# Values and states of a chunked recurrence in tiles of their own, one 128-partition state update for two heads

## The chip, the cores and the metric

One core of one Trainium2 chip runs the whole program in a single launch. The metric is the device time of the program in microseconds. Three plain runs of the kernel before are shown, and one profiled execution whose rows are quoted below.

## What is computed

The program is one mixer layer over 2048 tokens of width 1024: an adaptive norm, a wide input projection, three token mixers, an output projection with residual, and a last norm. The change touches the two mixers that are gated linear recurrences, with four heads each. GLA has keys of 64 and values of 128 per head, HGRN keys and values of 64. In chunks of 64 tokens each head does

```python
o_c = einsum('ts,sv->tv', scores, v_c) + einsum('td,dv->tv', q_c * exp(b_cum), state)
state = exp(b_last)[:, None] * state + einsum('sd,sv->dv', k_c * exp(b_last - b_cum), v_c)
```

where `b_cum` is the running sum of the log decay in the chunk and `scores` are the causal, decayed products of queries and keys. The third mixer, a stick-breaking attention, is not touched.

## The kernel before

The program runs in stages: the norm and the first projections, the value projections, the forget projections, the stick-breaking attention with projections woven in, the recurrences, and the output projection. All products are float32, or three products of split float32r parts. Between stages features, values and outputs lie in DRAM.

The recurrence stage (`gla_fast`, `gla_tail`, called from line 1057) works on pairs of heads: pairs 0 and 1 are GLA, pairs 2 and 3 HGRN, taken in this order. A pair's 2048 tokens go in four groups of 512, that is eight chunks, so there are 16 groups, called group 0 to group 15 below; groups 0 to 7 are GLA, 8 to 15 HGRN. Head h of a pair has its features on partitions 64h to 64h+63.

For one group SyncE loads the decays `bc`, queries `qt` and keys `kt`, the values `Vn` in token order, and the values once more into the tiles `W` (lines 884 to 886, 812, 821, 822). ScalarE makes exponentials (894, 897, 902). VectorE makes the scaled queries `eP` and keys `eN` (898, 899, 903), GpSimd the decayed keys `kd` (904). TensorE forms the scores `scp` (914) and transposes `kd` into `ptk` (833). ScalarE copies both out, as `S` and `KTt`, and GpSimd masks `S` into the tile `M` (921).

`W[h]` of a head has 128 partitions and one block per chunk: on its own 64 partitions the values of the chunk, on the other 64 the state at the chunk's start. `M[:, h]` matches it: on the own 64 partitions the masked scores, on the other 64 the queries times their decay, which VectorE writes there across the halves, one head at a time (906). So one product over 128 rows gives a chunk's output for one head (867). The state's increments `U` are 64-row products (844), in two PSUM tiles, one for even and one for odd chunks. VectorE carries the states from chunk to chunk, one instruction for each head and chunk (855), and the last chunk's goes into block 0 of the next group's `W`. The decay of a chunk stands on the swapped halves in `SX`, which two small copies (529 to 531) fill earlier, where the decays are made.

TensorE's order is written out by hand: for group i the scores and transposes, nine products of a gate projection as filler (257), the increments U of group i, nine fillers, the outputs o of group i-1. One of the two filler slots is

```python
            for i, tail in enumerate(gla_fast(GLA_ORDER, gp, gr_, pp, scp)):
                next(tail)
                run(fill, GLA_F[0])
                next(tail)
```

The order on the other engines and on the DMA queues comes from a planner that simulates the program. `U` has one buffer, so U of group i waits until the state updates of group i-1 have read it. `W` has two, so the values of group i+2 are loaded after the outputs of group i. A second, exact path (`gla_exact`) runs only when the decays are extreme; in these runs it is not entered.

Of the kernel before, what the change touches and what calls it, by code (L numbers as in the profile page):

```python
# [8 lines left out]
F32 = mybir.dt.float32  # L9
# [33 lines left out]
def hybrid_mixer_kernel(ctx, tc, x, c, w_ada, b_ada, w_in, w2, bg, gnw, lbl, hnw,  # L43
# [50 lines left out]
    SE = const.tile([P, 4, T // GTF, 3 * NBF], F32, name="SE")  # L94
    SX = const.tile([P, 4, T // GTF, NBF], F32, name="SX")
    ada_b = const.tile([P, 16], F32, name="ada_b")
# [423 lines left out]
    def decay_sums(pr, n, bc, g, s):  # L520

        b3 = v3(bc)
        sm, se = SM[:, pr, n, :], SE[:, pr, n, :]
        nc.vector.tensor_tensor_scan(bc, rmask, g, 0.0, op0=ALU.mult, op1=ALU.add)
        nc.vector.tensor_copy(sm[:, 0:2 * NBF].rearrange("p (e n) -> p n e", e=2),
                              b3[:, :, CB // 2 - 1:CB:CB // 2])
        nc.vector.tensor_tensor(sm[:, 2 * NBF:3 * NBF], sm[:, NBF:2 * NBF], sm[:, 0:NBF], op=ALU.subtract)
        fe[0] = nc.scalar.activation(se, sm, AF.Exp, scale=s)
        for h in range(2):
            nc.vector.tensor_copy(SX[(1 - h) * 64:(2 - h) * 64, pr, n, :],  # L530
                                  SE[h * 64:(h + 1) * 64, pr, n, NBF:2 * NBF])
# [272 lines left out]

    def load_values(pools, pr, g, GT, Wn):
        gla = pr < 2
# [6 lines left out]

        def new_w():
            return [pools.tile([P, NB, dv], F32, tag=f"W{h}", name=f"W{h}", bufs=2) for h in range(2)]
        W = Wn if Wn is not None else new_w()
        if Wn is None:
            nc.gpsimd.memset(W[0][64:128, 0, :], 0.0)
            nc.gpsimd.memset(W[1][0:64, 0, :], 0.0)
        vr = vcols.rearrange("(n p) d -> p n d", p=CB)  # L820
        nc.sync.dma_start(W[0][0:64], vr[:, :, 0:dv])
        nc.sync.dma_start(W[1][64:128], vr[:, :, dv:2 * dv])
        return Vn, W, new_w() if g + 1 < T // GT else None

    def gla_tail(gr_, pp, pr, g, GT, M, kd, dec, Vn, W, Wn):
        gla = pr < 2
# [13 lines left out]
        for n in range(NB):  # L840
            rs = slice((n % 2) * 64, (n % 2) * 64 + 64)
            for h in range(2):
                orow = slice((1 - h) * 64, (1 - h) * 64 + 64)
                mm(U[n % 2][orow, n // 2, :], KTt[rs, n // 2, h * 64:(h + 1) * 64],  # L844
                   Vn[rs, n // 2, h * dv:(h + 1) * dv], start=True, stop=True)
        for n in range(NB):
            for h in range(2):
                orow = slice((1 - h) * 64, (1 - h) * 64 + 64)
                if n + 1 < NB:
                    dst = W[h][orow, n + 1, :]  # L850
                elif Wn is not None:
                    dst = Wn[h][orow, 0, :]
                else:
                    continue
                nc.vector.scalar_tensor_tensor(dst, W[h][orow, n, :], dec[orow, n:n + 1],  # L855
                                               U[n % 2][orow, n // 2, :],
                                               op0=ALU.mult, op1=ALU.add)
        yield


        no = 2 if gla else 1
        o = pp.tile([P, no, GT], F32, tag="o", name="o")
        for n in range(NB):
            ns = slice(n * CB, (n + 1) * CB)
            for h in range(2):
                dst = o[:, h, ns] if gla else o[h * 64:(h + 1) * 64, 0, ns]
                mm(dst, W[h][:, n, :], M[:, h, ns], start=True, stop=True)
        for a in range(no):
# [5 lines left out]
    def gla_fast(pairs, gp, gr_, pp, scp):  # L874

        for pr in pairs:
            gla = pr < 2
            j = pr % 2
            s = 1.0 / 16.0 if gla else 1.0
            Wn = None  # L880
            for g in range(T // GTF):
# [4 lines left out]
                nc.sync.dma_start(kt, s_feat["ka" if gla else "kb"][j][:, tsl])  # L886
                Vn, W, Wn = load_values(gr_, pr, g, GTF, Wn)
# [4 lines left out]
                M = gr_.tile([P, 2, GTF], F32, tag="M", name="M", bufs=3)  # L892
                eP = gp.tile([P, GTF], F32, tag="eP", name="eP")
# [25 lines left out]
                for h in range(2):  # L919
                    hs = slice(h * 64, (h + 1) * 64)  # L920
                    nc.gpsimd.affine_select(v3(M[hs, h, :]), v3(S[hs]),
                                            pattern=[[0, NBF], [1, CB]], base=0,
                                            channel_multiplier=-1, compare_op=ALU.is_ge, fill=0.0)
                yield gla_tail(gr_, pp, pr, g, GTF, M, kd, SX[:, pr, g, :], Vn, W, Wn)

    def gla_exact(gp, pp):
# [4 lines left out]
        nc.sync.dma_start(mx, masks)  # L931
        M = gp.tile([P, 2, GT + NB], F32, name="M")
        nc.gpsimd.memset(M, 0.0)
        for pr in (2, 3, 0, 1):
            gla = pr < 2
            j = pr % 2
            s = 1.0 / 16.0 if gla else 1.0
            Wn = None
            for g in range(T // GT):
# [7 lines left out]
                nc.sync.dma_start(qt, s_feat["qa" if gla else "qb"][j][:, tsl])  # L947
                Vn, W, Wn = load_values(gp, pr, g, GT, Wn)
                if gla:
# [15 lines left out]
                def level(Xk, Xq, mi):  # L965
                    sc = pp.tile([P, NB, CB], F32, tag="sc", name="sc")
                    for n in range(NB):
                        for h in range(2):
                            hs = slice(h * 64, (h + 1) * 64)
                            ns = slice(n * CB, (n + 1) * CB)  # L970
                            mm(sc[hs, n, :], Xk[hs, ns], Xq[hs, ns], start=True, stop=True)
                    for h in range(2):
                        hs = slice(h * 64, (h + 1) * 64)
                        nc.vector.copy_predicated(
                            v3(M[hs, h, 0:GT]), mx[hs, mi:mi + 1, :].broadcast_to((64, NB, CB)), sc[hs])

# [21 lines left out]
                nc.vector.tensor_tensor(kt, kt, dd, op=ALU.mult)  # L998
                for h in range(2):
                    nc.vector.tensor_copy(M[(1 - h) * 64:(2 - h) * 64, h, :], Qs[h * 64:(h + 1) * 64, :])  # L1000
                dec = gp.tile([P, NB], F32, tag="dec", name="dec")
                for h in range(2):
                    orow = slice((1 - h) * 64, (2 - h) * 64)
                    nc.vector.tensor_copy(dec[orow], M[orow, h, GT:GT + NB])
                for _ in gla_tail(gp, pp, pr, g, GT, M, kt, dec, Vn, W, Wn):
                    pass
# [308 lines left out]
```

## Time and profile before

| | |
|---|---|
| three runs | 1293.93, 1297.98, 1299.10 us, median 1297.98 |
| the profiled execution | 1298.31 us, its span 1296.3 us |
| TensorE busy | 1216.6 us, 94% of the span |
| VectorE, ScalarE, GpSimd busy | 742.1, 471.7 and 164.7 us |
| mean granted TensorE clock | 0.977 of full speed |

The profiled execution took 2.0 us more than its span, and lies 0.3 us above the median of the runs. Busy shares are means over stages with different limits; the rows below look at the recurrence stage, from about 869 to 1066 us of the span, where all the changed instructions but two small copies run.

### The profile page before, as it was taken

Reading aid. Unit: us, or ns where it says so; the run is one execution under the profiler, and the core shown is the slowest. Engines: PE = TensorE matmul, PEld = TensorE weight load, DVE = VectorE, ACT = ScalarE, POOL = GpSimd, SP = SyncE. Lnnn points to the kernel's source line nnn. Section 1 sums busy time; section 2 is a strip of 40 time slices with the busy share of each in tenths; the row PEclk is TensorE's granted clock in tenths of the full one; section 3 lists DMA queues with packets and bytes.
Section 4 is the critical chain, followed back from the end, with each engine's and each line's share of the span. In section 5 each row is a group of like instructions: output and inputs, shape, how many; then the busy total and the mean of one; then the engine's idle time right before and its main releaser. Section 6 shows DMA issues by size and latency. Waiting matters only on the chain.

```text
span 1296.3 us, 22081 instructions
## 1 busy us (share of the span) xinstructions
PE 1216.6 (94%) x8682; PEld 987.1 (76%) x8682; DVE 742.1 (57%) x1268; ACT 471.7 (36%) x860; POOL 164.7 (13%) x197
## 2 busy tenths in 40 slices
PE   7999999999999899999999999998978896999997
PEld 6777789899997667777777776766867674777775
DVE  4856325700019873535546488867786667765652
ACT  3376423421124432323223344543333433253621
POOL 3210000000004300000000001012341312000000
PEclk8999999999999999999999999998989897999999
DMA  9765432422123331222333322127977657464621
GB/s 266 237 238 184 143 116 91 150 83 78 54 98 114 131 99 59 78 86 71 99 86 92 110 62 79 33 86 223 266 218 199 196 171 237 134 225 133 203 82 51
DMA packets 177566, 173.73 MB, mean 134 GB/s; under 512 B 39625, under 2 KB 131882, under 8 KB 177454
## 3 DMA queue, kind: packets, MB, share of 16 engines
q1 hardware_dynamic: 144970, 128.70, 33.6%
q10 hardware_dynamic: 32484, 43.54, 9.7%
q8 instruction: 70, 1.15, 0.4%
q14 instruction: 42, 0.34, 0.1%
HBM read 113.47 MB, written 58.73 MB: 133 GB/s over the span
## 4 chain that ended last, share of the span: by engine, by line
PE 61%; DVE 13%; DMA 7%; issue 5%; ACT 2%; POOL 1%; SPq 0%; ACTq 0%; POOLq 0%; DVEq 0%
PE acc L151 5%; PE av L747 5%; PE acc L153 5%; PE acc L152 5%; PE acc L163 4%; PE acc L165 4%; PE acc L164 4%; PE pt L735 4%; PE y L1191 4%; PE y L1189 4%; PE y L1190 4%; PE acc L257 4%; DVE W L855 2%; DVE f L731 2%; DMA kt<-s_kb 2%
## 5 line engine op out<-in xcount | busy, mean ns | idle before, releaser
L731 DVE TENSOR_TENSOR_SCAN f<-f 128x512 f32<-128x512 f32 (+3 forms) x160 | 169.9, 1091 | 21.6 <-ACT f L725 12.1
L151 PE MATMUL acc<-hTh,whi 128*128 128x512 f32 x400 | 161.9, 406 | 8.0 <-ACT st L182 3.8
L152 PE MATMUL acc<-hTl,whi 128*128 128x512 f32 x400 | 159.4, 398 | 0.0
L153 PE MATMUL acc<-hTh,wlo 128*128 128x512 f32 x400 | 159.2, 399 | 0.0
L163 PE MATMUL acc<-whi,hTh 128*128 128x256 f32 (+1 forms) x512 | 145.3, 284 | 1.6 <-ACT stt L190 1.6
L165 PE MATMUL acc<-whi,hTl 128*128 128x256 f32 (+1 forms) x512 | 144.9, 283 | 0.0
L164 PE MATMUL acc<-wlo,hTh 128*128 128x256 f32 (+1 forms) x512 | 144.8, 283 | 0.0
L257 PE MATMUL acc<-hTh,whi 128*128 128x512 f32 x240 | 104.3, 435 | 1.8 <-ACT hTh L241 1.8
L257 PE MATMUL acc<-hTl,whi 128*128 128x512 f32 x240 | 98.1, 409 | 3.9 <-DVE hTl L247 3.8
L1189 PE MATMUL y<-wh,hTh 128*128 128x512 f32 x256 | 101.5, 397 | 0.0
L1190 PE MATMUL y<-wl,hTh 128*128 128x512 f32 x256 | 101.1, 396 | 0.0
L1191 PE MATMUL y<-wh,hTl 128*128 128x512 f32 x256 | 99.9, 395 | 1.0 <-DVE hTl L1157 1.0
L725 ACT ACTIVATE f<-zt 128x512 f32<-128x512 f32 (+3 forms) x160 | 82.0, 537 | 50.5 <-DVE f L731 23.0
L257 PE MATMUL acc<-hTh,wlo 128*128 128x512 f32 x240 | 98.3, 410 | 1.0 <-POOL wlo L271 1.0
L151 PEld LDWEIGHTS acc<-hTh,whi 128*128 128x128 f32 x400 | 75.4, 189 | 29.8 <-ACT st L182 5.1
L163 PEld LDWEIGHTS acc<-whi,hTh 128*128 128x128 f32 x512 | 96.4, 188 | 2.0 <-ACT stt L190 1.8
L164 PEld LDWEIGHTS acc<-wlo,hTh 128*128 128x128 f32 x512 | 96.5, 188 | 0.1
L165 PEld LDWEIGHTS acc<-whi,hTl 128*128 128x128 f32 x512 | 96.4, 188 | 0.1
L153 PEld LDWEIGHTS acc<-hTh,wlo 128*128 128x128 f32 x400 | 75.4, 189 | 19.0 <-issue 1.4
L747 PE MATMUL av<-PT,V 128*64 128x128 f32 x960 | 89.0, 280 | 0.9 <-DVE PT L740 0.6
L152 PEld LDWEIGHTS acc<-hTl,whi 128*128 128x128 f32 x400 | 75.5, 189 | 17.0 <-issue 1.0
L855 DVE SCALAR_TENSOR_TENSOR W<-W,SX,U 64x128 f32<-64x128 f32 (+1 forms) x248 | 77.7, 313 | 18.0 <-PE U L844 6.9
(206 smaller groups left out, 2115.2 us busy)
## 6 DMA issues: line engine op xcount, KB each, us to landing
wraw<-in_w_in_dram SPq DMA_DIRECT2D x36, 512.0 KB, 5.1
xt<-in_x_dram SPq DMA_DIRECT2D x16, 512.0 KB, 5.2
wa<-in_w_ada_dram SPq DMA_DIRECT2D x16, 512.0 KB, 6.0
Q<-s_qc SPq DMA_DIRECT2D x64, 128.0 KB, 3.2
ot<-s_o SPq DMA_DIRECT2D x32, 256.0 KB, 3.3
gt<-s_gate SPq DMA_DIRECT2D x32, 256.0 KB, 4.2
r<-in_x_dram SPq DMA_DIRECT2D x16, 512.0 KB, 5.5
out_dram<-r SPq DMA_DIRECT2D x15, 512.0 KB, 2.8
```

Source lines behind the costliest of these rows:

```text
L151: mm(ps, hi[:, k, :], th[:, k, :], start=(k == 0), stop=False)
L152: mm(ps, hi[:, k, :], tl[:, k, :], start=False, stop=False)
L153: mm(ps, lo[:, k, :], th[:, k, :], start=False, stop=(k == KT - 1))
L163: mm(o, th[:, k, s], hi[:, k, 0:ncols], start=(k == 0), stop=False)
L164: mm(o, th[:, k, s], lo[:, k, 0:ncols], start=False, stop=False)
L165: mm(o, tl[:, k, s], hi[:, k, 0:ncols], start=False, stop=(k == KT - 1))
L257: mm(ps, a[:, k, :], b[:, k, :], start=(k == 0 and i == 0), stop=(k == KT - 1 and i == 2))
L731: nc.vector.tensor_tensor_scan(fr, fr, fr, carry[u], op0=ALU.mult, op1=ALU.bypass)
L747: last[0] = mm(av[u * 64:(u + 1) * 64, :], (Dd if diag else V)[J][:, b, :], PT[:, b, :], start=diag, stop=(J == 0 and b == 0))
L1189: mm(y, oh[:, k, us], wh, start=(k == 0), stop=False)
L1190: mm(y, oh[:, k, us], wl, start=False, stop=False)
L1191: mm(y, ol[:, k, us], wh, start=False, stop=(k == KT - 1))
```

## The change

The values of both heads lie in one tile `Vv` and the states of both heads in another, `St`; head h stands on partitions 64h to 64h+63 in each. One VectorE instruction updates both heads' states for a chunk. The masked scores are in a tile `Ms` and the decayed queries in `Qd`, again with both heads on their own partitions, so one VectorE instruction of 128 partitions writes `Qd`. The decay is read straight from `SE`, and `SX` with its copies is gone. A chunk's output for a head is now the sum of two 64-row products into the same PSUM block, values times scores and then state times queries. The increments `U` go to the head's own partitions instead of the other half. The loads keep their number and sizes.

```diff
@@ decay_sums
-        for h in range(2):
-            nc.vector.tensor_copy(SX[(1 - h) * 64:(2 - h) * 64, pr, n, :],
-                                  SE[h * 64:(h + 1) * 64, pr, n, NBF:2 * NBF])
@@ load_values
-        def new_w():
-            return [pools.tile([P, NB, dv], F32, tag=f"W{h}", name=f"W{h}", bufs=2) for h in range(2)]
-        W = Wn if Wn is not None else new_w()
-        if Wn is None:
-            nc.gpsimd.memset(W[0][64:128, 0, :], 0.0)
-            nc.gpsimd.memset(W[1][0:64, 0, :], 0.0)
+        def new_s():
+            return pools.tile([P, NB, dv], F32, tag="St", name="St", bufs=2)
+        St = Sn
+        if St is None:
+            St = new_s()
+            nc.gpsimd.memset(St[:, 0, :], 0.0)
+        Vv = pools.tile([P, NB, dv], F32, tag="Vv", name="Vv", bufs=2)
         vr = vcols.rearrange("(n p) d -> p n d", p=CB)
-        nc.sync.dma_start(W[0][0:64], vr[:, :, 0:dv])
-        nc.sync.dma_start(W[1][64:128], vr[:, :, dv:2 * dv])
-        return Vn, W, new_w() if g + 1 < T // GT else None
+        for h in range(2):
+            nc.sync.dma_start(Vv[h * 64:(h + 1) * 64], vr[:, :, h * dv:(h + 1) * dv])
+        return Vn, Vv, St, new_s() if g + 1 < T // GT else None
@@ gla_tail
             for h in range(2):
-                orow = slice((1 - h) * 64, (1 - h) * 64 + 64)
-                mm(U[n % 2][orow, n // 2, :], KTt[rs, n // 2, h * 64:(h + 1) * 64],
+                mm(U[n % 2][h * 64:(h + 1) * 64, n // 2, :], KTt[rs, n // 2, h * 64:(h + 1) * 64],
                    Vn[rs, n // 2, h * dv:(h + 1) * dv], start=True, stop=True)
         for n in range(NB):
-            for h in range(2):
-                orow = slice((1 - h) * 64, (1 - h) * 64 + 64)
-                if n + 1 < NB:
-                    dst = W[h][orow, n + 1, :]
-                elif Wn is not None:
-                    dst = Wn[h][orow, 0, :]
-                else:
-                    continue
-                nc.vector.scalar_tensor_tensor(dst, W[h][orow, n, :], dec[orow, n:n + 1],
-                                               U[n % 2][orow, n // 2, :],
-                                               op0=ALU.mult, op1=ALU.add)
+            if n + 1 < NB:
+                dst = St[:, n + 1, :]
+            elif Sn is not None:
+                dst = Sn[:, 0, :]
+            else:
+                continue
+            nc.vector.scalar_tensor_tensor(dst, St[:, n, :], dec[:, n:n + 1], U[n % 2][:, n // 2, :],
+                                           op0=ALU.mult, op1=ALU.add)
...
-        o = pp.tile([P, no, GT], F32, tag="o", name="o")
+        o = pp.tile([P, no, 512], F32, tag="o", name="o")[:, :, 0:GT]
         for n in range(NB):
             ns = slice(n * CB, (n + 1) * CB)
-            for h in range(2):
-                dst = o[:, h, ns] if gla else o[h * 64:(h + 1) * 64, 0, ns]
-                mm(dst, W[h][:, n, :], M[:, h, ns], start=True, stop=True)
+            for x, y, first in ((Vv, Ms, True), (St, Qd, False)):
+                for h in range(2):
+                    hs = slice(h * 64, (h + 1) * 64)
+                    dst = o[:, h, ns] if gla else o[hs, 0, ns]
+                    mm(dst, x[hs, n, :], y[hs, ns], start=first, stop=not first)
@@ gla_fast
-                for h in range(2):
-                    nc.vector.tensor_tensor(v3(M[(1 - h) * 64:(2 - h) * 64, h, :]),
-                                            v3(eP[h * 64:(h + 1) * 64]),
-                                            per_chunk(0)[h * 64:(h + 1) * 64], op=ALU.mult)
+                nc.vector.tensor_tensor(v3(Qd), v3(eP), per_chunk(0), op=ALU.mult)
...
-                    nc.gpsimd.affine_select(v3(M[hs, h, :]), v3(S[hs]),
+                    nc.gpsimd.affine_select(v3(Ms[hs]), v3(S[hs]),
...
-                yield gla_tail(gr_, pp, pr, g, GTF, M, kd, SX[:, pr, g, :], Vn, W, Wn)
+                yield gla_tail(gr_, pp, pr, g, GTF, Ms, Qd, kd, SE[:, pr, g, NBF:2 * NBF],
+                               Vn, Vv, St, Sn)
```

The exact path is rewritten in the same way.

## Rows read from the trace of the kernel before

**Rows 1.** The table by stretches: five engines' busy us (instructions), TensorE clock, DMA share, GB/s.

```profile
340.00:460.00 120.00, 113.09 (x621) 96.20 (x620) 67.53 (x107) 41.79 (x76) 25.92 (x18) 0.99 0.35 113
...
865.00:1066.00 201.00, 174.84 (x2485) 142.54 (x2484) 139.35 (x333) 66.25 (x114) 58.36 (x61) 0.94 0.71 209
```

**Rows 2.** The same table, finer, inside the recurrence stage.

```profile
884.80:904.60 19.80, 14.06 (x152) 11.52 (x151) 15.21 (x36) 4.08 (x7) 4.58 (x5) 0.74 0.70 215
904.60:937.20 32.60, 32.15 (x452) 27.60 (x451) 25.62 (x52) 10.99 (x19) 13.44 (x12) 1.00 0.85 247
937.20:956.70 19.50, 13.24 (x151) 10.97 (x150) 14.90 (x29) 5.99 (x10) 6.71 (x5) 0.82 0.73 223
991.70:1025.60 33.90, 27.28 (x451) 21.11 (x450) 23.15 (x64) 12.94 (x22) 10.76 (x10) 0.90 0.67 195
```

**Rows 3.** The waits of the recurrence stage: us in total, times, longest.

```profile
ACT kt L902 <- DMA kt<-s_kb: 30.8, 6, 8.4
...
PE U L844 <- issue: 10.4, 6, 6.2
...
PE U L844 <- DVE W L855: 6.9, 8, 3.0
...
PE U L844 <- ACT KTt L835: 4.9, 2, 2.8
...
PE U L844 <- ACT st L182: 1.8, 1, 1.8
```

**Rows 4.** VectorE over group 0's state updates: start, us, what, idle before.

```profile
884.19 4.90 DVE L855 SCALAR_TENSOR_TENSOR W<-W,SX,U 64x128 f32<-64x128 f32 x13
...
894.65 0.34 DVE L855 SCALAR_TENSOR_TENSOR W<-W,SX,U 64x128 f32<-64x128 f32 x1
```

**Rows 5.** TensorE at U of groups 1 and 5, and ScalarE's copy before group 5's.

```profile
891.39 0.69 PE L844 MATMUL U<-Vn,KTt 64*64 64x128 f32 x4 [2.78 <-ACT KTt L835]
895.04 1.97 PE L844 MATMUL U<-Vn,KTt 64*64 64x128 f32 x28 [2.96 <-DVE W L855]
...
947.23 2.68 PE L844 MATMUL U<-Vn,KTt 64*64 64x128 f32 x32 [6.25 <-issue]
...
943.42 0.59 ACT L835 COPY KTt<-ptk 128x512 f32<-128x512 f32 x1
```

**Rows 6.** VectorE's groups by shape, whole span: xcount, busy us, mean ns.

```profile
L855 DVE SCALAR_TENSOR_TENSOR W<-W,SX,U 64x128 f32<-64x128 f32 x124 | 43.0, 347 | 8.6 <-PE U L844 3.4 <-PE o L867 1.3
...
L855 DVE SCALAR_TENSOR_TENSOR W<-W,SX,U 64x64 f32<-64x64 f32 x124 | 34.7, 280 | 9.4 <-PE U L844 3.5 <-POOL M L921 2.0
...
L906 DVE TENSOR_TENSOR M<-eP,SE 64x512 f32<-64x512 f32 x32 | 25.5, 797 | 0.8
...
L530 DVE COPY SX<-SE 64x8 f32<-64x8 f32 x32 | 8.5, 265 | 0.8
...
L903 DVE TENSOR_TENSOR eP<-qt,eP 128x512 f32<-128x512 f32 x8 | 6.2, 776 | 16.6 <-ACT eP L894 16.6
```

**Rows 7.** VectorE in the first stage: five updates that each read the result just written.

```profile
32.38 2.56 DVE L312 SCALAR_TENSOR_TENSOR am<-wa,c_col,am 128x256 f32<-128x256 f32 x5
```

**Rows 8.** TensorE in a GLA iteration (groups 4 and 3): each matmul shows as two instructions.

```profile
926.65 1.09 PE L914 MATMUL scp<-eP,bc 64*32 64x64 f32 x64
...
930.03 0.40 PE L257 MATMUL acc<-hTl,whi 128*128 128x512 f32 x1
930.36 1.10 PE L844 MATMUL U<-Vn,KTt 64*64 64x128 f32 x32
...
933.59 3.68 PE L867 MATMUL o<-M,W 128*128 128x64 f32 x32
937.20 0.98 PE L914 MATMUL scp<-eP,bc 64*32 64x64 f32 x60
```

**Rows 9.** TensorE in HGRN iterations: U of group 8, outputs of group 13.

```profile
985.23 0.69 PE L844 MATMUL U<-Vn,KTt 64*64 64x64 f32 x32 [1.01 <-issue]
...
1050.61 1.15 PE L867 MATMUL o<-M,W 128*64 128x64 f32 x32
```

More of the change, by code (lines that the diff above doesn't have):

```diff
@@ L94, in hybrid_mixer_kernel @@
     SE = const.tile([P, 4, T // GTF, 3 * NBF], F32, name="SE")
-    SX = const.tile([P, 4, T // GTF, NBF], F32, name="SX")
     ada_b = const.tile([P, 16], F32, name="ada_b")
@@ L802, in hybrid_mixer_kernel, with load_values @@
     hpools[ORDER[2]].close()
-    def load_values(pools, pr, g, GT, Wn):
+    def load_values(pools, pr, g, GT, Sn):
         gla = pr < 2
@@ L812, in load_values, with gla_tail @@
         nc.sync.dma_start(Vn, vcols.rearrange("(b p) d -> p b d", p=P))
-        def new_w():
-            return [pools.tile([P, NB, dv], F32, tag=f"W{h}", name=f"W{h}", bufs=2) for h in range(2)]
-        W = Wn if Wn is not None else new_w()
-        if Wn is None:
-            nc.gpsimd.memset(W[0][64:128, 0, :], 0.0)
-            nc.gpsimd.memset(W[1][0:64, 0, :], 0.0)
+        def new_s():
[5 more added lines that the diff above has]
+        Vv = pools.tile([P, NB, dv], F32, tag="Vv", name="Vv", bufs=2)
         vr = vcols.rearrange("(n p) d -> p n d", p=CB)
-        nc.sync.dma_start(W[0][0:64], vr[:, :, 0:dv])
-        nc.sync.dma_start(W[1][64:128], vr[:, :, dv:2 * dv])
-        return Vn, W, new_w() if g + 1 < T // GT else None
-    def gla_tail(gr_, pp, pr, g, GT, M, kd, dec, Vn, W, Wn):
+        for h in range(2):
+            nc.sync.dma_start(Vv[h * 64:(h + 1) * 64], vr[:, :, h * dv:(h + 1) * dv])
+        return Vn, Vv, St, new_s() if g + 1 < T // GT else None
+    def gla_tail(gr_, pp, pr, g, GT, Ms, Qd, kd, dec, Vn, Vv, St, Sn):
         gla = pr < 2
@@ L879, in gla_fast @@
             s = 1.0 / 16.0 if gla else 1.0
-            Wn = None
+            Sn = None
             for g in range(T // GTF):
@@ L886, in gla_fast @@
                 nc.sync.dma_start(kt, s_feat["ka" if gla else "kb"][j][:, tsl])
-                Vn, W, Wn = load_values(gr_, pr, g, GTF, Wn)
+                Vn, Vv, St, Sn = load_values(gr_, pr, g, GTF, Sn)
                 def per_chunk(i):
                     return SE[:, pr, g, i * NBF:(i + 1) * NBF].unsqueeze(2).broadcast_to((P, NBF, CB))
-                M = gr_.tile([P, 2, GTF], F32, tag="M", name="M", bufs=3)
+                Ms, Qd = (gr_.tile([P, GTF], F32, tag=t, name=t, bufs=3) for t in ("Ms", "Qd"))
                 eP = gp.tile([P, GTF], F32, tag="eP", name="eP")
@@ L931, in gla_exact @@
         nc.sync.dma_start(mx, masks)
-        M = gp.tile([P, 2, GT + NB], F32, name="M")
-        nc.gpsimd.memset(M, 0.0)
+        Ms = gp.tile([P, GT], F32, name="Ms")
+        nc.gpsimd.memset(Ms, 0.0)
         for pr in (2, 3, 0, 1):
@@ L937, in gla_exact @@
             s = 1.0 / 16.0 if gla else 1.0
-            Wn = None
+            Sn = None
             for g in range(T // GT):
@@ L947, in gla_exact @@
                 nc.sync.dma_start(qt, s_feat["qa" if gla else "qb"][j][:, tsl])
-                Vn, W, Wn = load_values(gp, pr, g, GT, Wn)
+                Vn, Vv, St, Sn = load_values(gp, pr, g, GT, Sn)
                 if gla:
@@ L971, in level @@
                             mm(sc[hs, n, :], Xk[hs, ns], Xq[hs, ns], start=True, stop=True)
[L972 to L975, printed above, removed]
+                    nc.vector.copy_predicated(
+                        v3(Ms), mx[:, mi:mi + 1, :].broadcast_to((P, NB, CB)), sc)
                 for lv in range(6):
@@ L998, in gla_exact @@
                 nc.vector.tensor_tensor(kt, kt, dd, op=ALU.mult)
[L999 to L1005, printed above, removed]
+                for _ in gla_tail(gp, pp, pr, g, GT, Ms, Qs, kt, Qs[:, GT:GT + NB], Vn, Vv, St, Sn):
                     pass
```

## The prediction, made before the kernel was run

> **What bounds the kernel now.** I read the table by stretches first, to see where the changed work runs and which engine fills that stretch. All of it but the two small copies lies in the recurrence stage, 201 us in which TensorE is busy 174.8 us, VectorE 139.4 us and the DMA engines 71% [rows 1]. No engine is full, so the stage is cut further: three stretches keep TensorE waiting and show a granted clock below 1, 0.74, 0.82 and 0.90, and between the first two TensorE is busy for 32.15 of 32.60 us [rows 2]. So TensorE is the bound as long as nothing makes it wait, and the question is what makes it wait.
>
> The view of waits answers for the instruction at which TensorE stops most, the state increments U: 10.4 us named "issue", 6.9 us VectorE's state updates, 4.9 us ScalarE's copy KTt, 1.8 us another copy [rows 3]. The names need checking against the timeline. U of group 1 starts four instructions when KTt is there and then waits 2.96 us more [rows 5]; it goes on 0.05 us after the last update of group 0 ends at 894.65 + 0.34 [rows 4]. That is the single buffer of U: the next increments can't be written before the updates have read the old ones. The longest stop, 6.25 us before U of group 5, is in two parts. KTt ended at 944.01 [rows 5]; the remaining 947.23 - 944.01 = 3.2 us is again the updates. The 1.8 us I read the same way, since the copy named there feeds no U. So VectorE's updates cost TensorE 10.4 + 6.9 + 1.8 - 3.0 = 16.1 us, where 3.0 is the part of the 6.25 us before KTt was there. The reader should see that the largest part of this was named "issue".
>
> **The change, part by part.**
>
> *State updates.* 248 instructions become 124. A GLA one takes 347 ns, an HGRN one 280 ns on 64 partitions [rows 6]. Does 128 partitions cost more? 128x512 (776 ns) and 64x512 (797 ns) cost the same [rows 6], so no. Does a single chain cost more, now that each instruction reads what the one just before it wrote? Five such updates of 256 elements in the first stage take 2.56 us, 0.51 us each [rows 7], against 0.35 for 128 elements; the 0.16 us is about what 128 more elements cost by the 67 ns between 64 and 128 [rows 6], so at most 0.03 us per instruction, 8 x 0.03 = 0.24 us a group. The chain of a group falls from 16 x 0.38 (4.90 us for 13 of them [rows 4]) = 6.0 us to 3.0 + 0.24, about 3.2 us.
>
> *Decayed queries.* 32 instructions of 797 ns become 16 [rows 6]: 12.8 us less of VectorE in the stage, 0.8 us a group. With the updates (half of 43.0 + 34.7, 38.9 us), VectorE's 139 us become about 88.
>
> *The SX copies.* 8.5 us of VectorE [rows 6] go from earlier stages. TensorE is busy for 113.09 of 120 us in the stretch where most of VectorE's work on decays lies, and VectorE for 67.5 [rows 1], so I put this at nothing; TensorE's products hide it. Without that cover it would be a gain of at most 8.5 us.
>
> *Loads, masks, memsets.* As many loads with as many bytes, waiting for the same outputs of two groups before; as many masks; four memsets fewer on an engine that is busy 58 of 201 us [rows 1]. The last update of a group still waits for the outputs of the group before, through the two buffers of `St`. Nothing.
>
> *Output products, GLA.* 32 instructions of 128 rows take 3.68 us, 115 ns each [rows 8]. They become 64 of 64 rows with as many columns. If the two heads' products, which stand on different row halves, overlap, it is 64 x 115 / 2 = 3.68 us again. If they don't, 7.36. The nearest row is U: 32 products on four quarters of the array in 1.10 us, 34 ns each [rows 8], with twice the moving columns of `o`, less than a third of an `o` instruction. That can't be without overlap across row halves as well as column halves, so I take 3.68, and 7.36 as the bound.
>
> *Output products, HGRN.* 32 instructions in 1.15 us, 36 ns each, with the two heads on two column halves [rows 9]. They become 64, the heads on two diagonal quarters. From the `o` row, 64 x 36 = 2.3 us; from U of HGRN, 32 in 0.69 us or 21.6 ns on four quarters [rows 9], so 43 on two, 64 x 43 = 2.8 us; as low as 64 x 21.6 = 1.4 us if two quarters run as fast as four. I take 2.4: 8 x 1.25 = 10.0 us more TensorE work; bounds 2 and 13 us.
>
> Here a rule of the Trainium skill speaks against the change. The row shows scores of both heads, on both row halves, written into one PSUM bank at 17 ns an instruction [rows 8], faster than U's on four quarters. The page "TensorEngine Tiling (Array Packing)", section "Restrictions and Gotchas", says that different row tiles cannot access the same PSUM bank at the same time and that software has to keep them apart. HGRN's new products write both heads into one bank. Kept apart, they would go one by one; the row for the scores speaks against it, and the rival below gives the time.
>
> *Change of array shape.* U starts 0.33 us after the start of the last filler (930.03 to 930.36) where fillers follow each other every 0.23 us, so entering another tile shape costs some 0.1 us [rows 8]. The GLA outputs now do this too: 8 x 0.1 = 0.8 us.
>
> **The sum.** With the chain halved, VectorE finishes a group before the next U in nearly every place: of the 16.1 us I take 15.0 (bounds 8, if the planner puts updates behind waiting instructions, and 16.1). The clock: busy time times missing clock in the three slow stretches is 14.06 x 0.26 + 13.24 x 0.18 + 27.28 x 0.10 = 8.8 us [rows 2]. The stops get shorter but don't vanish, so I take 2.0 of it back (bounds 0 and 6). HGRN products +10.0, of which 2.0 fill waits that stay (KTt, 4.9 us [rows 3]). Shapes +0.8. When TensorE runs ahead, loads are late more often: ScalarE waits 30.8 us for HGRN's `kt` [rows 3], and a stage 7 us shorter asks the DMA engines for 7 / 201 = 3.5% more; I charge 1.2. Together 1298.3 - 15.0 - 2.0 + 10.0 - 2.0 + 0.8 + 1.2 = 1291.3, say 1291 us. The base is the profiled execution, 0.3 us above the median of the runs.
>
> **Rivals.**
>
> *Waits change their name.* The updates no longer stop U, but loads and KTt do. For it: the 30.8 us [rows 3], the DMA engines at 85% in the TensorE-bound stretch [rows 2]. Against it: KTt ends only 4.9 us of U's waits now [rows 3]. Half the 15.0 us returns, the rest pays the products: 1298.3 - 7.5 + 8.8 = 1300; 1295 to 1303.
>
> *GLA's 64-row products don't overlap* (the other side). Each group then needs 3.68 us more TensorE in the stretch where nothing else waits: 8 x 3.68 = 29.4 us. Some 8 us of this fill stops that TensorE has anyway. 1291.3 + 29.4 - 8 = 1313; 1308 to 1322. It decides from 7 / 8 = 0.9 us a group on, outputs of 4.6 us instead of 3.68. For it: no row of before has a tile of 64 rows and 128 columns. Against it: U.
>
> *HGRN's heads go one by one in their bank.* 64 x 86 ns (four times 21.6) = 5.5 us a group, 3.1 more than in the sum: 1291.3 + 25 = 1316. The rule cited above would make it so.
>
> *The planner orders VectorE, ScalarE or the loads worse,* so that an instruction that waits for a load stands ahead of the updates or of KTt, as before U of group 5, where 3.0 of the 6.25 us were no update's. One more such stop with its slow clock is about 10 us, twice that undoes the gain: 1301 to 1310.
>
> *More than counted.* HGRN's products take 1.4 us and the clock stays up: 1291.3 - 8 - 4 = 1279; 1275 to 1284.
>
> **Chances.** A change under 0.5% (6.5 us) can hardly be told from none here. The forecast: 0.50, its own range 1284 to 1298, of which 0.32 lies below 1291.5 and 0.18 above. Waits change their name 0.18 (same). GLA not overlapping 0.16, one bank 0.05, worse order 0.05 (slower). More than counted 0.06 (faster). So faster 0.38, same 0.36, slower 0.26. The range reaches from 1281 (most of "more than counted" left out) to 1316 (the top of the non-overlapping case left out).
>
> **What would show it.** State updates 128x128 of about 0.35 us, 124 of them, chain about 3.2 us a group; VectorE near 88 us in the stage. U waiting for VectorE under 3 us in total, "issue" before U down to what KTt explains. GLA outputs 3.7 us a group, HGRN's 2.4. The slow-clock stretches near 895 and 945 shorter, that around 1010 perhaps gone. The stage from the first filler to the last about 190 us instead of 197, the stages around it unmoved. The prediction is wrong if GLA's outputs take over 4.6 us, if U waits for KTt or for loads as long as it now waits for updates, or if the time moves outside this stage.

## The result and the profile after

The changed kernel takes 1315.7 us (median of four runs, 1314.25 to 1319.04), the kernel before 1298.5 us beside it. The ratio is 1.0144, with a 95% interval of 1.0113 to 1.0175: slower, where the forecast was 1291 us. The time lies just inside the range, which ended at 1316. The profiled execution took 1319.04 us with a span of 1317.2, so 20.9 us more of span than before. It is the longest of the four runs: the parts below explain 20.9 us, where the medians differ by 17.2.

I cut the two spans at the same four events of TensorE. The stage begins with the last attention product `av`, GLA's part goes from the scores `scp` of group 1 to those of group 8, HGRN's part from there to the first product of the norm that follows (`sqh`). These are the lines of the kernel before (one tile's instructions, then the timeline of TensorE):

```profile
L747 PE MATMUL av<-PT,V x960: 272/273/472, 463.4 to 869.0; 128*64 128x128 f32 x192
```

```profile
884.83 1.09 PE L914 MATMUL scp<-eP,bc 64*32 64x64 f32 x64
...
980.44 1.09 PE L914 MATMUL scp<-eP,kt 64*32 64x64 f32 x64
...
1071.91 0.40 PE L1134 MATMUL acc<-sqh,sel 128*8 128x512 f32 x1 [0.33 <-DVE fs L1086]
```

And the changed kernel, the same two views. The timeline also has the stops and, for later, the starts of two groups' output products and of the scores that follow them:

```profile
L743 PE MATMUL av<-PT,V x960: 272/273/324, 458.6 to 861.9; 128*64 128x128 f32 x192
```

```profile
877.70 1.09 PE L907 MATMUL scp<-eP,bc 64*32 64x64 f32 x64
...
896.93 0.44 PE L863 MATMUL o<-Ms,Vv 64*128 64x64 f32 x4
...
900.65 1.09 PE L907 MATMUL scp<-eP,bc 64*32 64x64 f32 x64
...
907.23 0.69 PE L841 MATMUL U<-Vn,KTt 64*64 64x128 f32 x4 [2.80 <-issue]
914.36 1.97 PE L841 MATMUL U<-Vn,KTt 64*64 64x128 f32 x28 [6.44 <-DVE St L850]
...
943.81 0.69 PE L841 MATMUL U<-Vn,KTt 64*64 64x128 f32 x4 [4.96 <-ACT KTt L833]
956.90 1.97 PE L841 MATMUL U<-Vn,KTt 64*64 64x128 f32 x28 [12.39 <-DVE St L850]
...
992.78 1.09 PE L907 MATMUL scp<-eP,kt 64*32 64x64 f32 x64
...
1025.36 0.33 PE L863 MATMUL o<-Ms,Vv 64*64 64x64 f32 x4
...
1027.37 1.09 PE L907 MATMUL scp<-eP,kt 64*32 64x64 f32 x64
...
1093.65 0.39 PE L1120 MATMUL acc<-sqh,sel 128*8 128x512 f32 x1 [2.48 <-DVE fs L1072]
```

The stage begins 869.0 - 861.9 = 7.1 us earlier, GLA's part takes 115.1 us instead of 95.6, HGRN's 100.9 instead of 91.5, and what follows 223.5 instead of 224.4: -7.1 + 19.5 + 9.4 - 0.9 = 20.9 us. So something was gained ahead of the stage, and far more was lost in GLA's part, where the forecast had its gain.

The work itself became what it was to be. VectorE's groups by shape (xcount, busy us, mean ns) answer to [rows 6]:

```profile
L850 DVE SCALAR_TENSOR_TENSOR St<-St,SE,U 128x128 f32<-128x128 f32 x62 | 21.5, 346 | 2.5
L850 DVE SCALAR_TENSOR_TENSOR St<-St,SE,U 128x64 f32<-128x64 f32 x62 | 17.4, 280 | 12.8 <-PE U L841 6.3 <-PE o L863 3.6 <-DVE St L850 0.5
...
L901 DVE TENSOR_TENSOR Qd<-eP,SE 128x512 f32<-128x512 f32 x16 | 12.6, 790 | 0.0
```

The waits of the stage answer to [rows 3]. By the names in this view TensorE waits longer at U for the updates than before, 19.1 us against 6.9 (16.1 as the prediction reads the names), though there are half as many. It waits longer for KTt too, 14.3 us against 4.9, and ScalarE waits 61.1 us for GLA's decays `bc`, 23.7 before:

```profile
ACT eP L890 <- DMA bc<-s_da: 61.1, 6, 18.2
...
DVE wh L1006 <- POOL wr L1003: 21.0, 3, 9.6
...
PE U L841 <- DVE St L850: 19.1, 3, 12.4
...
PE U L841 <- ACT KTt L833: 14.3, 5, 5.0
...
PE U L841 <- issue: 3.0, 2, 2.8
```

In the table by stretches, which answers to [rows 1, 2], VectorE fell to 85 us and the clock to 0.88. Two holes, a new one at 905 us and one at 937 us, deeper than the stop that the kernel before had there, have TensorE busy for 56% and 38% of the time (11.33 of 20.40 and 10.45 of 27.80 us) and a granted clock of 0.67 and 0.63; the stretch at 885, slow before, is now full:

```profile
865.00:1086.00 221.00, 181.91 (x2959) 147.72 (x2958) 85.20 (x191) 65.25 (x113) 54.24 (x57) 0.88 0.70 188
...
884.80:904.60 19.80, 19.63 (x330) 16.47 (x328) 8.56 (x16) 6.95 (x12) 4.60 (x5) 1.00 0.68 206
904.60:925.00 20.40, 11.33 (x157) 9.23 (x159) 8.68 (x15) 3.37 (x7) 6.30 (x4) 0.67 0.55 157
...
937.20:965.00 27.80, 10.45 (x95) 8.06 (x93) 10.78 (x17) 5.99 (x10) 7.36 (x6) 0.63 0.53 137
```

Why does U wait 6.44 us at 907.9 for an update? The timeline of VectorE (start, us, what, idle before):

```profile
904.43 2.70 DVE L850 SCALAR_TENSOR_TENSOR St<-St,SE,U 128x128 f32<-128x128 f32 x7
912.10 0.69 DVE L1006 CAST wh<-wr 128x1024 fp32r<-128x1024 f32 x1 [4.96 <-POOL wr L1003]
912.82 1.23 DVE L1007 TENSOR_TENSOR wl<-wr,wh 128x1024 fp32r<-128x1024 f32 x1
913.97 0.34 DVE L850 SCALAR_TENSOR_TENSOR St<-St,SE,U 128x128 f32<-128x128 f32 x1
```

Seven of group 2's eight updates run in one go. The eighth stands in VectorE's order behind two casts, `wh` and `wl`, of something else: the scaling of the output weights (`scale_wo`), which the next stage needs. The cast waits for GpSimd's multiplication of `wr`, and that, as GpSimd's timeline shows, for a load of `wr`, so TensorE waits at U of group 3 for a weight load:

```profile
909.72 2.34 POOL L1003 TENSOR_TENSOR wr<-wr,gb 128x1024 f32<-128x1024 f32 x1 [6.30 <-DMA wr<-in_w_out_dram]
```

In the source the scaling stands with groups 8 to 11; in both kernels the planner draws it forward into GLA's groups. But in the kernel before these casts waited for GpSimd 3.9 us in all, here 21.0. The next load of the scaling makes the second half of the story. This is SyncE's queue in the same kernel, issues only:

```profile
904.53 0.38 SPq L1002 DMA_DIRECT2D wr<-in_w_out_dram  x1
905.01 0.45 SPq L808 DMA_DIRECT2D Vn<-s_va  x1
914.11 0.37 SPq L1002 DMA_DIRECT2D wr<-in_w_out_dram  x1
914.58 1.26 SPq L820 DMA_DIRECT2D Vv<-s_va  x2
915.93 0.57 SPq L880 DMA_DIRECT2D bc<-s_da  x1
```

The second `wr` needs a buffer that `wl` gives back at 914.05. Until then the queue stands, with the values and `bc` of the next group behind it; ScalarE gets `bc` at 922.08:

```profile
922.08 0.63 ACT L890 ACTIVATE eP<-bc 128x512 f32<-128x512 f32 x1 [15.98 <-DMA bc<-s_da]
```

The same pattern comes back at 944 to 962 us, with the stop of 12.39 us at U of group 5: group 4's eighth update stands behind the next cast and starts at 956.51.

### The profile page after: what moved, and what is told of

The parts are those of the page before. It is cut to its first block, busy times and chain, and to the rows that moved or that the text cites. A ratio compares the mean times of both kernels' runs of the same rounds, so it can differ in the third digit from the quotient of the medians.

```text
span 1317.2 us, 22886 instructions
## 1 busy us (share of the span) xinstructions
PE 1225.4 (93%) x9194; PEld 992.0 (75%) x9194; DVE 676.5 (51%) x1096; ACT 470.5 (36%) x860; POOL 159.7 (12%) x193
## 4 chain that ended last, share of the span: by engine, by line
PE 59%; DMA 12%; DVE 8%; issue 5%; ACT 3%; POOL 2%; SPq 1%; ACTq 0%; POOLq 0%; DVEq 0%
PE av L743 5%; PE acc L150 5%; PE acc L152 5%; PE acc L151 5%; PE acc L162 5%; PE acc L164 5%; PE acc L163 5%; PE pt L731 4%; PE y L1175 4%; PE y L1176 4%; PE y L1177 4%; DMA bc<-s_da 2%; DMA kt<-s_kb 2%; PE acc L256 2%; DVE f L727 2%
## 5 line engine op out<-in xcount | busy, mean ns | idle before, releaser
L727 DVE TENSOR_TENSOR_SCAN f<-f 128x512 f32<-128x512 f32 (+3 forms) x160 | 169.8, 1090 | 22.2 <-ACT f L721 12.4
L731 PE MATMUL pt<-ident,f 128*128 128x128 f32 x544 | 86.4, 282 | 0.8 <-DVE f L727 0.7
```

What stands on the lines that cost most here:

```text
L727: nc.vector.tensor_tensor_scan(fr, fr, fr, carry[u], op0=ALU.mult, op1=ALU.bypass)
```

## The experiments

The theory after reading the traces: *the orders*, that is the order that the planner made of the new program, in two places. One is the scaling among the group's updates and loads. The other is *the load loop*: on SyncE's queue `bc` of group i+1 stands behind `qt` of group i+2, which needs a buffer that VectorE frees only in group i. The rival: *the products*, twice as many output instructions, cost the time, whatever the order. Each ratio is to runs of the kernel before on the same chip. Differences in us are of medians, some of them taken on different chips; on these the kernel before took 1298.0 to 1300.9 us.

**The scaling put in its place (a_pin).** The two pins hold the scaling's instructions behind the group's own loads and state updates.

```diff
@@ load_values
-            nc.sync.dma_start(Vv[h * 64:(h + 1) * 64], vr[:, :, h * dv:(h + 1) * dv])
+            pin[0] = nc.sync.dma_start(Vv[h * 64:(h + 1) * 64], vr[:, :, h * dv:(h + 1) * dv])
@@ gla_tail
-            nc.vector.scalar_tensor_tensor(dst, St[:, n, :], ...
+            pin[1] = nc.vector.scalar_tensor_tensor(dst, St[:, n, :], ...
@@ the loop over the groups
-                next(ws, None)
+                with tc.issue_after(pin[0].ins), tc.issue_after(pin[1].ins):
+                    next(ws, None)
```

> The changed kernel, with only the place of the output-weight scaling altered: its loads stand on SyncE's queue behind the loads of the group in which the program text has them (groups 8 to 11), and its casts on VectorE behind that group's state updates; the planner had drawn both forward into groups 2 to 6. Order theory (the loss comes from scaling loads and casts that stand ahead of the group loads and of a group's last state update): U waits for state updates under 4 us in total instead of 19, the waits for bc of GLA fall from 61 us to under 35, the recurrence stage falls from some 226 us to 195 or less, the whole to 1285 us (1278 to 1295). Product theory (the doubled output products cost it): the stage keeps its length but for a few us, 1310 to 1318. Load theory (the group loads are late whatever the order): the waits for updates go, those for bc stay over 50 us, 1300 to 1312.

Measured: 1301.1 us, ratio 1.0020 [1.0003, 1.0038]. So 1315.7 - 1301.1 = 14.6 of the 17.2 us come back from an order alone. GLA's part falls to 86.7 us, and U's waits for VectorE from 19.1 to 0.4 us; those for KTt stay:

```profile
PE U L843 <- ACT KTt L835: 14.4, 7, 4.0
...
PE U L843 <- DVE St L852: 0.4, 1, 0.4
```

HGRN's part, where the scaling now is, takes 108.4. The waits for updates went as the order theory had it, but the time did not: it lies above that theory's 1278 to 1295 and in the load theory's 1300 to 1312. ScalarE still waits 36.6 us for GLA's `bc`, and 38.9 for HGRN's.

**The same pins in the kernel before (b_pin).**

> The kernel before, with the same alteration of the place of the output-weight scaling and nothing else. Order theory: the kernel before suffered little from the scaling's place (part of the one stop of 6.25 us in group 5), so it gains at most 8 us: 1290 to 1300, and its U still waits 10 us or more for state updates, since the chain of 16 updates stays. If this kernel gains as much as the changed one from the pinning (over 20 us), the place of the scaling is not what sets the two apart. Product and load theories say nothing of it: 1295 to 1302.

Measured: 1300.6 us, 1.0007 [0.9988, 1.0025]. That is just above the order theory's 1290 to 1300 and inside the 1295 to 1302 of the others. The pins by themselves gain nothing; the loss that they undo was the changed kernel's.

**Without the product of states and queries (a_half).** Outputs hold values times scores only.

```diff
-            for x, y, first in ((Vv, Ms, True), (St, Qd, False)):
+            for x, y, first in ((Vv, Ms, True),):
...
-                    mm(dst, x[hs, n, :], y[hs, ns], start=first, stop=not first)
+                    mm(dst, x[hs, n, :], y[hs, ns], start=True, stop=True)
```

> The changed kernel without the second of the two accumulating output products (state times queries is left out, so the outputs lack that part); the order on the other engines is the planner's again. Product theory: TensorE loses 256 of 512 output instruction pairs, 1.9 us in a GLA and 1.0 us in an HGRN group, 23 us in all, and the time falls by 18 us or more, to under 1298 us. Order theory: the long stops before U stay, at most 10 us are gained, 1303 to 1318 us.

Measured: 1296.4 us, one run. That is 19 us less, a time that the product theory had (under 1298) and the order theory had not. Yet long stops stay, as the order theory had it, and the run doesn't tell the two apart: without these products the planner made another order too. U waits for "issue" 21.7 us here, up to 11.2 at once, instead of 3.0, and the waits for GLA's `bc` fell from 61.1 to 35.1 us. The run a_pinhalf repeats it with the two pins.

**The copies into SX put back, unread (a_sx).**

```diff
+        for h in range(2):
+            nc.vector.tensor_copy(SX[(1 - h) * 64:(2 - h) * 64, pr, n, :],
+                                  SE[h * 64:(h + 1) * 64, pr, n, NBF:2 * NBF])
```

> The changed kernel with the small copies into the swapped decay tile put back (nobody reads them). In the changed kernel the recurrence stage starts about 7 us earlier than before. If the copies' absence gives these 7 us, the first filler of the stage moves from 862 back to 867 to 870 us; if the earlier start is only another order of the stages ahead, it stays within 2 us of 862. Neither theory of the loss in the recurrence stage says anything of this.

Measured: 1323.3 us, one run; the last `av` is at 868.4 instead of 861.9 us:

```profile
L747 PE MATMUL av<-PT,V x960: 272/273/324, 463.7 to 868.4; 128*64 128x128 f32 x192
```

So 6.5 of the 7.1 us ahead of the stage are the copies' doing, by their own time or by the order without them.

**Feature loads in sequence (a_ord), and the same in the kernel before (b_ord).** To a_pin and b_pin:

```diff
-                nc.sync.dma_start(bc, s_feat["da" if gla else "db"][j][:, tsl])
-                nc.sync.dma_start(qt, s_feat["qa" if gla else "qb"][j][:, tsl])
-                nc.sync.dma_start(kt, s_feat["ka" if gla else "kb"][j][:, tsl])
+                with tc.issue_after(front[0].ins) if front[0] is not None else ExitStack():
+                    nc.sync.dma_start(bc, s_feat["da" if gla else "db"][j][:, tsl])
+                    nc.sync.dma_start(qt, s_feat["qa" if gla else "qb"][j][:, tsl])
+                    front[0] = nc.sync.dma_start(kt, s_feat["ka" if gla else "kb"][j][:, tsl])
```

> The changed kernel with the weight scaling's loads behind a group's own loads and its casts behind a group's state updates (as in the run a_pin, 1301.1 us), and besides with the loads of each group's bc, qt and kt kept in the order of the groups on SyncE's queue, so that bc of group i+1 stands ahead of qt of group i+2, which waits for VectorE. Theory 'a load loop': the GLA groups' period falls from about 12.7 to TensorE's 10.7 us, ScalarE's waits for bc from 75 us to under 20, and the time is about 1286 us (1280 to 1293). Rival 'the products cost it' (twice as many output products fill TensorE, whatever the order): no change, 1298 to 1304.

> The kernel before with the same two orders, weight scaling and feature loads. Theory 'a load loop' in the changed kernel only: little, 1293 to 1300 us, since the state updates' chain and TensorE set the period here. Rival 'the feature loads cost both kernels the same': as large a gain as the changed kernel has from it, about 1286 us.

Measured: a_ord 1289.8 us, 0.9916 [0.9886, 0.9945]; b_ord 1293.0 us, 0.9948 [0.9927, 0.9969]. The loop is real. In a_pin SyncE issues `qt` as soon as VectorE's `eP` ends (902.41 + 0.69 us), and only then the values and `bc`; ScalarE, in the last line below, has `bc` at 914.24, 8.8 us after its issue, and VectorE's next `eP` starts at 914.90:

```profile
903.13 0.32 SPq L883 DMA_DIRECT2D qt<-s_qa  x1
903.54 0.39 SPq L810 DMA_DIRECT2D Vn<-s_va  x1
904.03 1.33 SPq L822 DMA_DIRECT2D Vv<-s_va  x2
905.47 0.87 SPq L882 DMA_DIRECT2D bc<-s_da  x1
```

```profile
902.41 0.69 DVE L896 SCALAR_TENSOR_TENSOR eP<-qt,eP 128x512 f32<-128x512 f32 x1 [8.30 <-ACT eP L892]
...
914.90 0.69 DVE L896 SCALAR_TENSOR_TENSOR eP<-qt,eP 128x512 f32<-128x512 f32 x1 [5.03 <-ACT eP L892]
```

```profile
914.24 0.63 ACT L892 ACTIVATE eP<-bc 128x512 f32<-128x512 f32 x1 [6.69 <-DMA bc<-s_da]
```

So one turn of the loop takes 12.5 us, longer than TensorE's group of 10.7 us. In a_ord `bc` goes ahead of `qt` and of the next `Vn`, and ScalarE has it 5.4 us after its issue:

```profile
904.94 0.56 SPq L885 DMA_DIRECT2D bc<-s_da  x1
...
906.10 0.42 SPq L886 DMA_DIRECT2D qt<-s_qa  x1
```

```profile
910.31 0.63 ACT L895 ACTIVATE eP<-bc 128x512 f32<-128x512 f32 x1 [4.42 <-DMA bc<-s_da]
```

GLA's part falls from 86.7 to 77.5 us, with four of its seven groups 10.74 us apart. As much is gained in HGRN's part (108.4 to 99.5), which these lines don't show. Two details missed: the waits for `bc` fell to 48.7 us, not under 20 (in GLA they no longer cost TensorE: in a_ord3 below they are 1.8 us, and GLA's part is no shorter), and b_ord gained 7.6 us against b_pin, where "little" was expected; its time lies at the lower edge of that theory's 1293 to 1300. The kernel before had the loop too, only less of it.

**Half the products, with the pins (a_pinhalf).** The edit of a_half, made to a_pin.

> The run a_pin without the product of states and queries, so that outputs hold values times scores only, and TensorE has 512 output products of 64 rows fewer. The orders of loads are otherwise as in a_pin. Theory 'a load loop': GLA groups keep a period of about 12 us, the gain against a_pin is at most 10 us and lies mostly in the HGRN groups (1291 to 1300). Rival 'the products cost it': half of 3.7 us in each of 8 groups and half of 2.0 in each of the other 8, with the clock's share, some 20 us: about 1281.

Measured: 1289.3 us, one run, 11.9 less than a_pin. GLA's part, which holds the outputs of seven GLA groups, loses 4.1 us (86.7 to 82.6) of the 7 x 3.72 / 2 = 13.0 us of products taken out. HGRN's part, with the eighth, loses 9.4 of 1.9 + 8 x 2.0 / 2 = 9.9 us. So in GLA the products were mostly hidden behind the loop, as the load loop theory has it, and in HGRN they cost nearly their full time; the total gain is 2 us more than that theory's bound, and the time 8 us above the rival's 1281.

**The order of the loads without the pins (a_ordonly).** The edit of a_ord, made to the changed kernel as it was.

> The changed kernel with the order of the feature loads alone: bc, qt and kt of a group behind those of the group before on SyncE's queue; the weight scaling stays where the planner puts it. Theory 'two independent orders': the scaling's 14.6 us stay lost and the load loop's 11 us come back, so about 1304 us (1299 to 1309). Rival 'one order': with the loads in sequence the planner draws the scaling elsewhere, or the scaling's stops only showed because loads were late, 1287 to 1295.

Measured: 1301.3 us, 1.0034 [1.0017, 1.0052], as the theory of two independent orders has it. Both stops at the scaling are still there, at the same groups, as TensorE's timeline of this run shows:

```profile
914.16 1.97 PE L843 MATMUL U<-Vn,KTt 64*64 64x128 f32 x28 [7.33 <-DVE St L852]
...
952.93 1.97 PE L843 MATMUL U<-Vn,KTt 64*64 64x128 f32 x28 [10.47 <-DVE St L852]
```

GLA's part is 106.4 us (8.7 less than in the changed kernel), HGRN's 88.0 (12.9 less). So these are two costs, nearly independent: either order alone brings some 14.5 us back, both together (a_ord) 26; by the ratios it is 16, 14 and 30.

**Three buffers for the features (a_ord3, b_ord3).** To a_ord and b_ord:

```diff
-                bc, qt, kt = (gp.tile([P, GTF], F32, tag=t, name=t) for t in ("bc", "qt", "kt"))
+                bc, qt, kt = (gp.tile([P, GTF], F32, tag=t, name=t, bufs=3) for t in ("bc", "qt", "kt"))
```

> The run a_ord with three buffers each for bc, qt and kt, so that qt of group i+2 need not wait for VectorE's reading of group i. Theory 'a load loop': what is left of waits for bc goes, 0 to 6 us below a_ord. Rival: no further change, since TensorE then sets the period.

> The kernel before with both orders and three buffers each for bc, qt and kt, as the run a_ord3 is for the changed kernel. Theory 'the change is worth its time once loads don't set the period': the state updates' long chain stays, so 1289 to 1295 us, and the changed kernel is 8 to 13 us faster at equal order and buffers. Rival 'the gain lies in the buffers alone': about 1282 us, as a_ord3.

Measured: a_ord3 1281.8 us, 0.9844 [0.9816, 0.9873], the fastest kernel of this study; b_ord3 1285.2 us, 0.9897 [0.9878, 0.9916]. a_ord3 lies 8.0 us below a_ord, more than the 0 to 6 expected. Neither extreme held for b_ord3: the buffers help the kernel before as well, and at equal order and buffers the change is worth 0.9897 - 0.9844 = 0.5% by the ratios, 3.4 us or 0.3% by the medians, not 8 to 13 us. The stage in both, by the table by stretches (a_ord3, then b_ord3):

```profile
864.50:1056.10 191.60, 178.30 (x2996) 146.26 (x2993) 86.80 (x196) 68.40 (x117) 54.10 (x57) 0.98 0.80 230
```

```profile
869.70:1056.80 187.10, 173.53 (x2485) 141.89 (x2482) 142.80 (x335) 68.66 (x117) 59.54 (x61) 0.95 0.78 231
```

In b_ord3 one stop that waits for the updates is left, at U of group 1, as in the kernel before; a_ord3 has none:

```profile
894.78 1.97 PE L848 MATMUL U<-Vn,KTt 64*64 64x128 f32 x28 [3.41 <-DVE W L859]
```

**The copies again, in the fast order (a_ord3_sx).** The edit of a_sx, made to a_ord3.

> The run a_ord3 with the 32 copies into SX put back, whose result nobody reads. Theory 'the copies were on the path ahead of the stage': the recurrence stage starts about 6.5 us later and the time is 1287 to 1290 us. Rival 'hidden by TensorE's products' (the prediction's step): within 2 us of a_ord3.

Measured: 1285.6 us, 0.9907 [0.9880, 0.9933]. `av` ends at 870.0 us, 5.5 later than in a_ord3. In the profiled execution the stage made it up (first norm product at 1056.1 us in both), in the median it is 3.8 us slower, and 8 us by the ratios. So neither the theory's 5 to 8 us nor the rival's 2 is settled: the later start is shown, and what of it reaches the end lies between 0 and 8 us.

This run also shows what the rest of the change is worth. It has everything that a_ord3 changes but the missing copies, and b_ord3 has the same orders and buffers with nothing changed: 1285.6 us and 0.9907 against 1285.2 us and 0.9897, on the same chip. So as far as these runs can tell, the gain at equal order is that of the 32 copies; the updates for both heads and the split products together gain nothing that shows.

**GLA changed, HGRN as before (mix3).** To a_ord3: HGRN's groups use the 128-row products and the update for each head again, in the same buffers, and SX with its copies for those two pairs.

> The run a_ord3 with the HGRN pairs put back to the form of before (128-row output products, one state update for each head, SX and its copies for those two pairs alone), the GLA pairs changed. Theory 'the change pays in GLA and costs in HGRN': a_ord3's GLA groups 1 to 7 (77.6 us), b_ord3's way from group 8 to the first norm product (89.1 instead of 98.2 us), half of the copies' 5.2 us: 1281.8 - 9.1 + 2.6 = about 1275 us (1272 to 1279). Rival 'the end of the stage is set by loads and the weight scaling, not by the products': 1280 to 1285.

Measured: 1286.9 us, 0.9911 [0.9892, 0.9930]: the theory missed, and the rival's 1280 to 1285 too. Its stage is, with that of a_ord3_sx, the shortest of all (186.3 us; GLA 76.7, HGRN 93.8) and ends at 1054.4 us, before a_ord3's, but HGRN's part has two stops of 3.69 and 4.17 us at U, "issue" and KTt, and the four runs spread from 1282.6 to 1288.8. The parts of two kernels can't be added: each new program is planned anew.

The parts of the stage in us, from TensorE's timelines:

| | start | GLA part | HGRN part | median |
|---|---|---|---|---|
| before | 869.0 | 95.6 | 91.5 | 1298.5 |
| after | 861.9 | 115.1 | 100.9 | 1315.7 |
| a_pin | 863.6 | 86.7 | 108.4 | 1301.1 |
| b_pin | 870.2 | 91.2 | 97.9 | 1300.6 |
| a_ordonly | 863.7 | 106.4 | 88.0 | 1301.3 |
| a_ord | 864.2 | 77.5 | 99.5 | 1289.8 |
| b_ord | 870.9 | 86.9 | 90.7 | 1293.0 |
| a_ord3 | 864.5 | 77.6 | 98.2 | 1281.8 |
| b_ord3 | 869.7 | 82.2 | 89.1 | 1285.2 |
| a_ord3_sx | 870.0 | 77.2 | 93.1 | 1285.6 |
| mix3 | 868.1 | 76.7 | 93.8 | 1286.9 |

## Why the prediction was wrong

**State updates and decayed queries: right.** 124 updates of 346 and 280 ns, no dearer on 128 partitions, in one chain of 2.70 us for seven, so 3.1 for eight (3.2 predicted), and VectorE at 85 us in the stage (88).

**Output products: right in kind.** GLA's 64 instructions take 900.65 - 896.93 = 3.72 us (3.68 predicted), so the rival "GLA's 64-row products don't overlap" falls. HGRN's take 1027.37 - 1025.36 = 2.0 us against 2.4. Between undisturbed HGRN groups scores start 8.64 us apart in a_ord3 and 7.71 in b_ord3, so the 10.0 us of the sum were 8 x 0.93 = 7.4. Between undisturbed GLA groups it is 10.74 and 10.55, so the +0.8 for the change of array shape was at most 8 x 0.19 = 1.5. The rival "HGRN's heads go one by one in their bank" falls at its price: 31 ns an instruction, where the prediction's estimate for one by one was 86. That estimate takes it that U's four quarters run fully side by side; no run has one quarter alone, so whether the two heads' products ever ran at once is not shown. The Trainium skill's rule ("TensorEngine Tiling (Array Packing)", "Restrictions and Gotchas", that different row tiles can't access one PSUM bank at once) costs no time that shows here, where the two heads write different halves of a bank's partitions.

**The step that failed: the -15.0 us for U's waits.** It said that with the chain halved VectorE finishes a group before the next U "in nearly every place", and its worst bound was still a gain of 8. That holds for how long the updates take and says nothing of where they stand. The kernel before already shows the difference. Between the two lines of [rows 4] VectorE ran:

```profile
890.44 0.72 DVE L855 SCALAR_TENSOR_TENSOR W<-W,SX,U 64x128 f32<-64x128 f32 x2
891.20 0.92 DVE L899 TENSOR_TENSOR bc<-kt,bc 128x512 f32<-128x512 f32 x1
892.14 2.47 DVE L906 TENSOR_TENSOR M<-eP,SE 64x512 f32<-64x512 f32 x2
```

Fifteen of group 0's sixteen updates were done at 891.16, 0.2 us before U of group 1 started. The last one stood behind 3.4 us of other work, and the stop of 2.96 us came from its place, not from the chain's 6.0 us. In the changed kernel the last update of two groups stood behind casts that wait for a weight load, and U's waits for VectorE grew to 19.1 us by name; all of U's waits went from 24.0 to 38.1 us, where the sum took 15.0 off. The pins took the waits for VectorE away and brought 14.6 us. With orders and buffers equal, U waits 9.4 us in b_ord3 and 5.4 in a_ord3, so the term is worth 4.0 us. The prediction had the stops behind casts as a rival, "the planner orders VectorE, ScalarE or the loads worse", with the mechanism as it came (an instruction that waits for a load ahead of the updates) and a price of 10 us a stop. There were two stops, of 6.4 and 12.4 us, and the late `bc` behind each, and the time came out above its 1301 to 1310; the chance given to it was 0.05. That was the second fault: the planner makes its order by simulating the whole program, and the change took 124 updates, 16 multiplications, four memsets and 32 copies out of it and doubled 256 output products. That the order would come out as good as before was assumed without a reason, and [rows 5] already showed one stop of which a part was no update's.

**The loads: +1.2 us, measured some 4.** The step charged a stage that needs 3.5% more of the DMA engines. What counted was again order: `bc` behind `qt` and the values in one queue. Putting them in sequence gave 1301.1 - 1289.8 = 11.3 us in the changed kernel and 1300.6 - 1293.0 = 7.6 in the kernel before, so 3.7 us came with the change and 7.6 were in the base. With the scaling's stops out of the way, a_pin is the rival "Waits change their name" as it was written: 1301.1 us where it said 1300, and U waiting for KTt 14.4 us instead of 4.9. So the forecast would have failed without those two stops too.

**The SX copies: put at nothing, worth 5 to 7 us of an earlier start.** The cover named, TensorE busy for 113 of 120 us [rows 1], didn't hide them; the bound of 8.5 us did hold. The prediction's own sign, "if the time moves outside this stage", came true here. With the copies (a_sx, a_ord3_sx) TensorE waits 5.3 and 3.2 us (3.8 and 3.2 in the kernel before) for two ScalarE copies `st` at the projections ahead of the first `av`, without them (the changed kernel, a_ord3) 1.0 and 2.1: 5.4 us, about what the start moves. Whether it moves by the copies' own time or by the order that the planner makes with them stays open.

**The clock: -2.0 us, it went the other way.** Busy time times missing clock over the stage is 10.7 us before (177.6 us at 0.94, from the first filler to the first norm product) and 20.9 after (190.0 us at 0.89). The slow stretch at 885 went, as predicted; two longer ones came with the new stops.

**The sum in a calm order.** a_ord3 against b_ord3 shows what the change itself does. It starts 5.2 us earlier, GLA's part takes 4.6 us less (the stop at U of group 1 gone) and HGRN's 9.1 us more. That is 0.7 us of profile, 3.4 in the medians and 6.9 by the ratios. The forecast's 7 us of gain is at the upper end of that, but that is luck, for it comes by other terms: 14.6 of the 24.0 us that U waits before are also gone in b_ord3, by order and buffers, without any change to the updates, and a_ord3_sx puts what is left down to the copies. What stays open is why the runs of one program here spread by up to 11 us (a_ord, 1283.8 to 1294.8), which limits how finely such a pair can be told apart.

## What to carry to other kernels

Where a planner orders the queues, a change of any operation is a change of all orders: price it as two things, the work and a new draw of the order, and compare both versions with the order of the critical loads and updates held before judging the change. When an instruction on the bounding engine waits, look at what stands ahead of its producer on the producer's engine, not at how long the producer takes; here 0.34 us of update cost 6 and 12 us behind a cast that waited for a load. And loads that wait for a buffer don't belong in a queue ahead of loads that the present stage waits for: a few lines of order and buffers for the feature loads gave the kernel before 1.0%, the rewrite 0.3 to 0.5% on top of that.

## What the runs showed of the hardware

- Splitting a product of 128 rows and 128 columns into two of 64 rows on the two row halves cost TensorE no time: 64 instructions of 64 columns each in 3.72 us, 58 ns apart, where 32 of the 128-row form take 3.68 us, 115 ns apart [rows 8]. That is what full overlap of the two halves would give; the overlap itself is inferred.
- Two heads' products on diagonal quarters, both into one PSUM bank on different partition halves, go 31 ns apart.
- A load of one and the same size was used later after its issue where more had gone out just ahead of it: `bc` of groups 3 to 6 7.8 to 9.5 us after its issue in a_pin, where `qt` and the values go out in the 1.9 to 3.5 us ahead of it, and 5.4 to 6.9 us in a_ord, where only `Vv` does. In all of these ScalarE was waiting for it.
